# First layer's activations kept by token residue mod 4 for the strided attention groups

## The chip, the cores and the metric

The kernel runs on one core of a Trainium2 chip. The metric is the device time of one execution in microseconds (us). Three runs of the kernel before the change took 2244.28, 2245.24 and 2247.7 us; their median, 2245.24 us, is the time that the change is compared with. One further execution was profiled, and all rows of the trace shown below come from that one.

On the core, TensorE (PE) multiplies matrices: it first loads a 128x128 block as weights (PEld, the stationary operand) and then streams the columns of the other operand through it. VectorE (DVE), ScalarE (ACT) and GpSimd (POOL) work element by element on 128 partitions, and DMA queues move data; SyncE (SP) and ACT issue the DMAs of this kernel.

## The reference

Two decoder layers on 1024 tokens of width 1024, all in float32. The first layer is a dilated sliding-window attention, the second a gated linear recurrence; both also attend into 256 memory tokens and have a gate:

```python
for l in range(DEPTH):                       # DEPTH = 2
    h = rms_norm(x, norm_gain[l])
    cols = h @ w_in[l]                       # q, k, v | memory query | gate
    mix = dilated_mixer(...) if l % 2 == 0 else hgrn2_mixer(...)
    mem_out = memory_cross_attention(q_mem, mem, ...)
    y = jnp.concatenate([mix, mem_out], axis=-1) * jax.nn.silu(gate)
    x = x + y @ w_out
```

In the dilated mixer there are three groups of eight heads, (window, dilation) = (128, 1), (512, 4), (2048, 16). Each group has its own q, k and v columns. A token t of a group sees t, t - d, t - 2d and so on, with d the dilation, up to the window; the three outputs of a head are merged by their softmax denominators. A group of dilation d can be computed apart for each residue of the token number mod d.

## The kernel before

**Numbers and operands.** A float32 product is made of three TensorE passes: each operand is split into a rounded part `hi` and a rest `lo`, and the kernel adds hi·hi, hi·lo and lo·hi. So each 128x128 block of activations meets 512 columns of weights in three matmuls (lines 222 to 224 in `project`). The normed activations are held transposed in two tiles of 128 x 8 x 1024 floats, `hhi` and `hlo`: partition and block k together are the feature, and the last axis is the token, in natural order. In the projections of this layer a block of 128 tokens is the stationary operand, and the weights (`wh`, `wl`) stream.

**The stages of the first layer.** The rows of `x` are loaded in eight tiles of 128 tokens, normed, transposed and split into `hhi` and `hlo` (`put_hT`). Then follow the first half of the gate columns (`gate_chunk(0)`), the memory keys and values, the memory queries with their attention (`mem_queries`, `mem_attend`), and four gate slices for the memory part (`gate_mem`). Their results go to scratch arrays in DRAM: `gate_scr` by token rows, `om_scr` and `gatem_scr` as features by tokens. Then come the six attention steps, (Q, g) for two halves of the heads Q and the groups g = 2, 1, 0 in this order: each projects k, v and q for 8 tiles of 128 tokens and attends, with a tile's attention running beside the projections of later tiles. At the end `out_proj` reads the scratch arrays back, multiplies by the gate, and projects.

**Which tokens a tile holds.** `tile_rows` says it: group 0 takes 128 neighbouring tokens, group 1 every 4th token of a half, group 2 every 8th token of all (its dilation of 16 is met by a mask inside the tile). `lhs_group` turns this into slices of `hhi` and `hlo`, so that a weight load for group 1 reads floats at a step of 4, for group 2 at a step of 8.

**What sets the order.** The program is written step by step as above; the layer that builds the instruction streams places each engine's instructions by a simulated timeline and by the buffers that come free, so that neighbouring steps interleave on an engine. The streams are then fixed: each engine runs its own list in order and waits for semaphores. Weights are loaded in pieces by SP, copied to `wh` by ACT and to `wl` by DVE (`piece`, lines 182 and 184). Three PSUM tiles `acc` take the projections. The second-layer part, from line 847 on, is not touched.

**Lines that matter below.** Line 222 to 224: the three projection matmuls; 266 to 271: `head_norm`; 277: the transposes of q and k; 702: scores of groups 1 and 2; 708 and 710: mask, minimum and exponential; 715: transposes of the probabilities; 717: their copy `pts`; 721: products with v; 373, 438 and 410: stores to `om_scr`, `gatem_scr` and `gate_scr`; 805: the loads of the first two in `out_proj`.

## Time and profile before

| what | value |
|---|---|
| median of three runs | 2245.24 us (2244.28 to 2247.7) |
| the profiled execution, its own time | 2248.89 us |
| its span in the trace | 2247.0 us |
| PE busy | 2200.2 us, 98% of the span |
| DVE busy | 1056.9 us, 47% |
| ACT busy | 735.0 us, 33% |
| POOL busy | 504.5 us, 22% |
| data moved by DMA | 185.58 MB, 83 GB/s on average |

The profiled execution is 3.65 us longer than the median of the runs. The time line of the first layer, in us from the start of the span: norm and transposes to about 40, first gate half, memory keys and values to about 170, memory queries to 251, the six attention steps from 240 to 1225, output projection to about 1490. A busy share says how much of the time an engine had an instruction in flight; for PE, whose matmuls overlap, it is the spacing of the starts that tells how fast it runs.

### The profile page before, as it was taken

What the parts mean: (1) busy time and instruction counts of PE and PEld (TensorE: products, weight loads), DVE (VectorE), ACT (ScalarE), POOL (GpSimd) and SP (SyncE); (2) the same over time, 40 slices, a digit from 0 to 9 for tenths busy, and PEclk for the clock granted to TensorE, in tenths of its full rate; (3) what the DMA queues carried; (4) which work ended last, traced back from release to release, by engine and by line L of the source; (5) the groups of instructions that cost most, each with busy time, mean ns of one, the idle gap of its engine ahead of it and who ended that gap; (6) DMA issues with size and microseconds to landing.
All of it is one profiled execution on the core that took longest, in us unless ns stands there. A gap on an engine that the chain in (4) does not pass through costs nothing.

```text
span 2247.0 us, 29432 instructions
## 1 busy us (share of the span) xinstructions
PE 2200.2 (98%) x11288; PEld 1952.4 (87%) x11288; DVE 1056.9 (47%) x2198; ACT 735.0 (33%) x1447; POOL 504.5 (22%) x720
## 2 busy tenths in 40 slices
PE   8999999999999999999999998889999999999999
PEld 6778999999888999999988877678888888888787
DVE  5646213413424422422433559752657772776443
ACT  5436323423423322422422531232542222222211
POOL 2813212212212222222222125511200000000221
PEclk9999999999999999999999999999999999999999
DMA  5542111211211211211211286531311111112733
GB/s 192 161 141 62 52 38 43 72 38 49 66 38 46 64 43 41 69 43 43 67 43 43 72 268 197 173 101 42 90 49 50 48 60 54 57 48 66 245 121 113
DMA packets 152667, 185.58 MB, mean 83 GB/s; under 512 B 17104, under 2 KB 88016, under 8 KB 152528
## 3 DMA queue, kind: packets, MB, share of 16 engines
q1 hardware_dynamic: 115200, 140.50, 20.8%
q10 hardware_dynamic: 37328, 43.20, 5.4%
q8 instruction: 90, 1.47, 0.3%
q14 instruction: 49, 0.40, 0.1%
HBM read 140.48 MB, written 43.19 MB: 82 GB/s over the span
## 4 chain that ended last, share of the span: by engine, by line
PE 87%; DMA 5%; DVE 4%; ACT 1%; issue 1%; POOL 1%; SPq 0%; ACTq 0%; DVEq 0%; POOLq 0%
PE acc L222 16%; PE acc L224 16%; PE acc L223 16%; PE acc L422 5%; PE acc L423 5%; PE acc L424 5%; PE acc L498 3%; PE acc L496 3%; PE po L721 3%; PE acc L497 3%; PE pt L277 2%; DMA ol<-o_scr 2%; PE s L702 2%; PE pt L949 1%; PE s L949 1%; PE pt L715 1%
## 5 line engine op out<-in xcount | busy, mean ns | idle before, releaser
L222 PE MATMUL acc<-wh,hhi 128*128 128x512 f32 x1536 | 614.6, 404 | 4.4 <-DVE qn L271 1.5
L223 PE MATMUL acc<-wl,hhi 128*128 128x512 f32 x1536 | 617.8, 403 | 0.0
L224 PE MATMUL acc<-wh,hlo 128*128 128x512 f32 x1536 | 617.1, 404 | 0.0
L222 PEld LDWEIGHTS acc<-wh,hhi 128*128 128x128 f32 x1536 | 389.7, 254 | 36.4 <-DVE qn L271 1.6
L156 POOL TENSOR_TENSOR rr<-rv,nhalf 128x4 f32<-128x4 f32 (+1 forms) x152 | 147.6, 972 | 1204.9 <-DVE rv L154 1196.0
L223 PEld LDWEIGHTS acc<-wl,hhi 128*128 128x128 f32 x1536 | 390.6, 254 | 29.8 <-DVE wl L184 0.4
L224 PEld LDWEIGHTS acc<-wh,hlo 128*128 128x128 f32 x1536 | 389.8, 254 | 30.0
L184 DVE TENSOR_TENSOR wl<-raw,wh 128x1024 fp32r<-128x1024 f32 x168 | 213.1, 1269 | 403.7 <-ACT wh L147 403.1
L147 ACT ACTIVATE wh<-raw 128x1024 fp32r<-128x1024 f32 x168 | 177.7, 1059 | 216.7 <-PE acc L224 61.9
L424 PE MATMUL acc<-hhi,wl 128*128 128x512 f32 x512 | 204.1, 399 | 0.0
L423 PE MATMUL acc<-hlo,wh 128*128 128x512 f32 x512 | 203.9, 398 | 0.0
L422 PE MATMUL acc<-hhi,wh 128*128 128x512 f32 x512 | 203.1, 397 | 0.6 <-DVE ol L435 0.6
L268 DVE TENSOR_REDUCE ss<-sq 128x4 f32<-128x512 f32 x116 | 79.4, 684 | 189.1 <-ACT sq L266 188.9
L496 PE MATMUL acc<-wh,yhi 128*128 128x512 f32 x384 | 156.9, 412 | 11.5 <-DVE x L503 7.6
L497 PE MATMUL acc<-wl,yhi 128*128 128x512 f32 x384 | 154.8, 403 | 4.2 <-DVE wl L184 4.2
L498 PE MATMUL acc<-wh,ylo 128*128 128x512 f32 x384 | 153.4, 404 | 0.2 <-POOL ylo L1140 0.2
L266 ACT ACTIVATE sq<-acc 128x512 f32<-128x512 f32 x116 | 68.9, 594 | 204.3 <-PE acc L224 198.0
L710 ACT ACTIVATE pa<-pa,st 128x128 f32<-128x128 f32 (+1 forms) x192 | 84.4, 441 | 109.2 <-DVE st L708 109.2
L717 DVE COPY pts<-pt 128x256 f32<-128x256 f32 (+1 forms) x96 | 51.8, 544 | 143.8 <-PE pt L715 143.8
L271 DVE TENSOR_TENSOR qn<-acc,rr 128x512 f32<-128x512 f32 x116 | 79.2, 687 | 82.1 <-PE pt L277 47.4
L422 PEld LDWEIGHTS acc<-hhi,wh 128*128 128x128 f32 x512 | 96.3, 188 | 19.0 <-DVE ol L435 0.8
L423 PEld LDWEIGHTS acc<-hlo,wh 128*128 128x128 f32 x512 | 96.3, 188 | 18.6
(220 smaller groups left out, 3133.6 us busy)
## 6 DMA issues: line engine op xcount, KB each, us to landing
raw<-in_w_in_a_dram SPq DMA_DIRECT2D x88, 512.0 KB, 3.9
raw<-in_w_in_b_dram SPq DMA_DIRECT2D x40, 512.0 KB, 3.9
o_scr<-os ACTq DMA_DIRECT2D x48, 256.0 KB, 2.0
ol<-o_scr SPq DMA_DIRECT2D x16, 768.0 KB, 6.1
raw<-in_w_mem_kv_dram SPq DMA_DIRECT2D x16, 512.0 KB, 4.2
raw<-in_w_out_a_dram SPq DMA_DIRECT2D x12, 512.0 KB, 5.2
raw<-in_w_out_b_dram SPq DMA_DIRECT2D x12, 512.0 KB, 4.2
gt<-gateb_scr SPq DMA_DIRECT2D x24, 256.0 KB, 5.2
```

The lines of the kernel that those rows point to most:

```text
L147: A.activation(dst, src, AF.Copy)
L156: G.tensor_tensor(r[:], v[:], nhalf[:, :n], op=OP.pow)
L184: W_LO.tensor_tensor(lo[:], raw[:], hi[:].bitcast(F32), op=OP.subtract)
L222: T.matmul(ps, hi, wh[:, j, :], start=k == 0, stop=False)
L223: T.matmul(ps, hi, wl[:, j, :], start=False, stop=False)
L224: T.matmul(ps, lo, wh[:, j, :], start=False, stop=k == n - 1)
L422: T.matmul(ps[:], wh[:, k, :], mh, start=k == 0, stop=False)
L423: T.matmul(ps[:], wh[:, k, :], ml, start=False, stop=False)
L424: T.matmul(ps[:], wl[:, k, :], mh, start=False, stop=k == 7)
L496: T.matmul(pss[ch][:], hi[:, k, :], wh[:, j, :], start=k == 0, stop=False)
L497: T.matmul(pss[ch][:], hi[:, k, :], wl[:, j, :], start=False, stop=False)
L498: T.matmul(pss[ch][:], lo[:, k, :], wh[:, j, :], start=False, stop=k == 3)
```

## The change

The transposed activations are written in another order of tokens. The rows of `x` are loaded by residue: tile m now holds 128 tokens of residue m // 2 mod 4 (`residue_rows`), so that position 256 r + j of `hhi` and `hlo` is token 4 j + r. With that, a tile of group 1 is 128 neighbouring positions, and a tile of group 2 is every second position. Three things follow from the other order:

- The first gate half is stored to token rows at a step of 4. The memory output and the memory gate are features by tokens; they are stored with the residue inside each 128 tokens (`by_residue`), in runs of 32 floats, two stores for each one of before. `y_a` puts them into natural order when it splits them into hi and lo, by a strided write.
- The six attention steps run in the order (0, 2), (0, 1), (1, 2), (1, 1), (0, 0), (1, 0), so both steps of group 0 come last.
- Before the first of these two, `natural_order` rearranges `hhi` (by ACT) and `hlo` (by DVE) to natural order: eight blocks of 128x1024 each, the first two into the room of the tile `kl` that is not yet in use, the others each into the place two blocks before, and the two in `kl` back into the last two places. 20 copies in all. `ROLLED` has group 0 use the blocks in the order in which they become ready.

```diff
-    def project(pss, lhss, pieces, after=None):
+    def project(pss, lhss, pieces, after=None, order=None):
...
-                    k = 2 * i + j
-                    hi, lo = lhs(k)
+                    at = 2 * i + j
+                    hi, lo = lhs(2 * (order or range(4))[i] + j)
...
+    def by_residue(scr, r):
+        return scr.rearrange("p (a r j) -> p r a j", a=8, r=4)[:, r]
...
+        if scr is om_scr:
+            for hh in range(2):
+                r0 = (2 * hp + hh) * 128
+                SQ.dma_start(by_residue(scr[r0:r0 + 128], mp), os[:, hh].rearrange("p (a j) -> p a j", j=32))
+            return
...
+    def natural_order(spare):
+        for n, e in (("hi", A), ("lo", V)):
+            slots = [hts[n][:, k, :] for k in range(8)]
+            rooms = [spare[n, k] for k in range(2)] + slots
+            for k in range(8):
+                copy(e, rooms[k].rearrange("p (j r) -> p j r", r=4), slots[k].rearrange("p (r j) -> p j r", r=4))
+            for k in range(2):
+                copy(e, slots[6 + k], spare[n, k])
+        hts["at"] = [6, 7, 0, 1, 2, 3, 4, 5]
...
     def lhs_group(g, m):
-        r0, st = tile_rows(g, m)
-        return lambda k: (hts["hi"][:, k, r0:r0 + 127 * st + 1:st], hts["lo"][:, k, r0:r0 + 127 * st + 1:st])
+        if g == 0:
+            return lhs_natural(m)
+        if g == 1:
+            return lhs_natural(m % 4 * 2 + m // 4)
+        r0 = 256 * (m % 4) + m // 4
+        return lambda k: [hT(n, k)[:, r0:r0 + 255:2] for n in ("hi", "lo")]
+
+    def residue_rows(scr, m):
+        return rows(scr, 1, m // 2 + 4 * (m % 2))
...
-    for Q in range(2):
-        for g in (2, 1, 0):
+    group_order = (0, 2), (0, 1), (1, 2), (1, 1), (0, 0), (1, 0)
+    for Q, g in group_order:
...
-                first = Y.dma_start(xt[:], x[m * 128:(m + 1) * 128, :])
+                first = Y.dma_start(xt[:], residue_rows(x, m))
...
+            for Q, g in group_order:
+                if (Q, g) == (0, 0):
+                    t = kpool.tile([128, NT, 4, 128], F32R, name="kl")[:].rearrange("p (k m) h t -> p k (m h t)", k=4)
+                    natural_order({(n, k): t[:, 2 * i + k, :] for i, n in enumerate(("hi", "lo")) for k in range(2)})
...
-                y = y.rearrange("p (k t) -> p k t", k=4)
-                copy(A, hi[:], y)
-                V.tensor_sub(lo[:], y, hi[:].bitcast(F32))
+                y = y.rearrange("p (k r j) -> p k j r", k=4, r=4)
+                hi, lo = (t[:].rearrange("p k (j r) -> p k j r", r=4) for t in (hi, lo))
+                copy(A, hi, y)
+                V.tensor_sub(lo, y, hi.bitcast(F32))
```

**How the instructions move.** Three places are shown. The lists are those of the engines' own streams; `x3` behind a row is three of its kind in a row.

The first place is ACT at the end of the memory attention, where the attention steps begin. Here `os` is the memory output of two heads, `qn` in this place a gate slice, `sq` the squares for the first k tile. Before:

```order
L373 DMA om_scr<-os 128x2x256
L147 ACTIVATE pmh<-pt 128x4x128
L438 DMA gatem_scr<-qn 128x512
L147 ACTIVATE os<-po 128x512
L373 DMA om_scr<-os 128x2x256
L266 ACTIVATE sq<-acc 128x512 x3
L740 ACTIVATE kT<-pt,gqk 128x512 x2
```

With the change:

```order
L382 DMA om_scr<-os 1024x1x32 x2
L147 ACTIVATE pmh<-pt 128x4x128
L477 DMA gatem_scr<-qn 1024x1x32 x2
L147 ACTIVATE kl<-hhi 128x1024 x2
L147 ACTIVATE os<-po 128x512
L382 DMA om_scr<-os 1024x1x32 x2
L268 ACTIVATE sq<-acc 128x512 x3
L784 ACTIVATE kT<-pt,gqk 128x512 x2
```

The first two of the eight block copies stand here, at the very start of the attention steps and not at their fifth; each store has become two of 1024 runs of 32 floats. DVE has its two copies `kl<-hlo` at the same place.

The second place is DVE where a step of group 1 ends and a step of group 0 begins. `ISA` is the masked minimum of line 708 (749 in the changed kernel), `pts` the probabilities on their way back to PE, `wl` a weight piece. Before:

```order
L717 COPY pts<-pt 128x256
L708 ISA pa,st<-s,masks 128x128
L708 ISA st 128x1
L708 ISA pa,st<-s,masks 128x128
L708 ISA st 128x1
L268 TENSOR_REDUCE ss_4889<-sq 128x4
L154 TENSOR_SCALAR rv_4891<-ss_4889 128x4
L184 TENSOR_TENSOR wl<-raw,wh 128x1024
L268 TENSOR_REDUCE ss_4960<-sq 128x4
L154 TENSOR_SCALAR rv_4962<-ss_4960 128x4
L184 TENSOR_TENSOR wl<-raw,wh 128x1024
```

With the change:

```order
L149 COPY hlo<-hlo 128x1024 x5
L758 COPY pts<-pt 128x256
L184 TENSOR_TENSOR wl<-raw,wh 128x1024
L749 ISA pa,st<-s,masks 128x128
...
L149 COPY hlo<-hlo 128x1024
L758 COPY pts<-pt 128x256
L749 ISA pa,st<-s,masks 128x128
...
L149 COPY hlo<-kl 128x1024
L184 TENSOR_TENSOR wl<-raw,wh 128x1024
L149 COPY hlo<-kl 128x1024
```

Where rows are left out stand one more pair of minimum and read-out each time. Eight copies now stand between the attention's and the weights' rows, five of them in one block. ACT has its eight, `hhi<-hhi` and `hhi<-kl`, spread between exponentials and weight pieces.

The third place is PE at the same point, in the first k tile of the step (0, 0) of the changed kernel, with what each instruction waits for. Numbers tell tiles of one name apart: `wl_7065` is the weight piece that DVE makes behind the five copies, `wl_7569` the one between the last two.

```order
L224 MATMUL acc_7838<-wh_7063,hhi_122 128x512 [waits Activation_49]
L762 MATMUL po_7336<-vv_6935,pts_7348 128x128 [waits Activation_49]
L762 MATMUL po_7336<-vv_6935,pts_7348 128x128
L225 MATMUL acc_7838<-wl_7065,hhi_122 128x512 [waits DVE_49]
L226 MATMUL acc_7838<-wh_7063,hlo_123 128x512
L762 MATMUL po_7336<-vv_6935,pts_7363 128x128 [waits DVE_49]
L762 MATMUL po_7336<-vv_6935,pts_7363 128x128
L224 MATMUL acc_7838<-wh_7063,hhi_122 128x512 [waits Activation_49]
L225 MATMUL acc_7838<-wl_7065,hhi_122 128x512
L226 MATMUL acc_7838<-wh_7063,hlo_123 128x512
L224 MATMUL acc_7838<-wh_7567,hhi_122 128x512 [waits Activation_49]
L225 MATMUL acc_7838<-wl_7569,hhi_122 128x512 [waits DVE_49]
```

In the same place of the kernel before, the same kinds of rows stand with waits for the weight pieces alone. SP's list is the same row for row; from within the last attention step on, the lists of the other engines are the same too, so the output projection and the second layer keep their order on every engine.

More of the change, by code (lines that the diff above doesn't have):

```diff
@@ L185, in piece, with plan_chunk @@
         return v(hi[:]), v(lo[:])
-    def plan_chunk(key, w, c0, r0=0, nr=D):
+    ROLLED = (1, 2, 3, 0)
+    def plan_chunk(key, w, c0, r0=0, nr=D, order=None):
         v = w[r0:r0 + nr, c0:c0 + 512].rearrange("(k p) n -> p k n", p=128)
-        for i in range(nr // 256):
+        for i in order or range(nr // 256):
             plan.append((key, v[:, 2 * i:2 * i + 2, :]))
@@ L219, in project, with project_tiles @@
                 for j in range(2):
-                    k = 2 * i + j
-                    hi, lo = lhs(k)
-                    T.matmul(ps, hi, wh[:, j, :], start=k == 0, stop=False)
+                    at = 2 * i + j
+                    hi, lo = lhs(2 * (order or range(4))[i] + j)
+                    T.matmul(ps, hi, wh[:, j, :], start=at == 0, stop=False)
                     T.matmul(ps, hi, wl[:, j, :], start=False, stop=False)
-                    T.matmul(ps, lo, wh[:, j, :], start=False, stop=k == n - 1)
+                    T.matmul(ps, lo, wh[:, j, :], start=False, stop=at == n - 1)
             if after:
                 after(i)
-    def project_tiles(key, lhs, each):
+    def project_tiles(key, lhs, each, order=None):
         W = take(key, 4)
@@ L427, in feature_proj, with gate_slice @@
         return pss
-    def gate_slice(key, scr, pool=gs, name="os", gain=None):
+    def gate_slice(key, scr, pool=gs, name="os", gain=None, mem_a=False):
         for hf, ps in enumerate(feature_proj(key)):
@@ L437, in gate_slice @@
                 V.scalar_tensor_tensor(sg, sg, gain, ps[:], op0=OP.mult, op1=OP.mult)
-            SQ.dma_start(scr[:, hf * 512:(hf + 1) * 512], sg)
+            if mem_a:
+                for i in range(2):
+                    SQ.dma_start(by_residue(scr, 2 * hf + i), sg[:, i * 256:(i + 1) * 256].rearrange("p (a j) -> p a j", j=32))
+            else:
+                SQ.dma_start(scr[:, hf * 512:(hf + 1) * 512], sg)
     og = const.tile([128, 1], F32, name="og")
@@ new lines, in trunk_kernel, with each_k, each_v, each_q @@
+            for Q, g in group_order:
+                if (Q, g) == (0, 0):
+                    t = kpool.tile([128, NT, 4, 128], F32R, name="kl")[:].rearrange("p (k m) h t -> p k (m h t)", k=4)
+                    natural_order({(n, k): t[:, 2 * i + k, :] for i, n in enumerate(("hi", "lo")) for k in range(2)})
+                order = None if g else ROLLED
+                kT = kpool.tile([128, NT, 4, 128], F32 if g else F32R, name="kT")
+                kl = None if g else kpool.tile([128, NT, 4, 128], F32R, name="kl")
+                vv, ql = {}, {}
+                lhs = lambda m: lhs_group(g, m)
+                def each_k(m, ps):
+                    n = head_norm(ps, ap_)
+                    rotary(n, g, 1, m)
+                    t = heads_T(n)
+                    A.activation(kT[:, m], t[:], AF.Copy, scale=gqk[:, g:g + 1])
+                    if g == 0:
+                        V.scalar_tensor_tensor(kl[:, m], t[:], gqk[:, g:g + 1], kT[:, m].bitcast(F32),
+                                               op0=OP.mult, op1=OP.subtract)
+                def each_v(m, ps):
+                    vv[m] = vring.tile([128, 512], F32, name="vv")
+                    copy(A, vv[m][:], ps)
+                def each_q(m, ps):
+                    n = head_norm(ps, ap_)
+                    rotary(n, g, 0, m)
+                    t = heads_T(n)
+                    q = at_.tile([128, 4, 128], F32 if g else F32R, name="qT")
+                    if g:
+                        copy(A, q[:], t[:])
+                    else:
+                        ql[m] = at_.tile([128, 4, 128], F32R, name="ql", bufs=1)
+                        split_evac(q[:], ql[m][:], t[:])
+                    if waiting:
+                        attend(Q, g, *waiting.pop(), kT, kl, vv)
+                    waiting.append((m, q, ql.get(m)))
+                project_tiles(("k", Q, g), lhs, each_k, order)
+                project_tiles(("v", Q, g), lhs, each_v, order)
+                waiting = []
+                project_tiles(("q", Q, g), lhs, each_q, order)
+                attend(Q, g, *waiting.pop(), kT, kl, vv)
```

59 lines of the change are left out of this document (14 added, 45 removed).

## The prediction

> **What bounds the kernel now.** I read the page's shares first, then the waits of the stretch in which the change works (240 to 1225 us, the six attention steps), then the spacing of PE's matmuls there.
>
> ```profile
> PE 2200.2 (98%) x11288; PEld 1952.4 (87%) x11288; DVE 1056.9 (47%) x2198; ACT 735.0 (33%) x1447; POOL 504.5 (22%) x720
> PEclk9999999999999999999999999999999999999999
> ...
> DVE wl L184 <- ACT wh L147: 268.4, 64, 37.1
> ACT sq L266 <- PE acc L224: 175.9, 63, 6.8
> DVE pts L717 <- PE pt L715: 126.9, 51, 5.3
> PEld acc L222 <- DVE qn L271: 1.6, 3, 0.7
> PE acc L222 <- DVE qn L271: 1.5, 5, 0.4
> ```
>
> The first two lines are of the page, the others of the waits from 240 to 1225 us (who waited for whom, us in total, times, longest). ACT and DVE wait for PE for hundreds of us; PE waits for anybody for some 3 us in 985. So in these steps the time is the sum of PE's own instructions, the granted clock is full, and only what changes PE's spacing, or makes PE wait, counts. DVE, ACT, POOL and the DMAs have room, and what is added to them is free until PE waits for it.
>
> How fast PE runs differs between the groups. The weight loads of line 222 in three stretches of pure projection (820 to 860 us: group 2, step of 8; 480 to 520: group 1, step of 4; 650 to 690: group 0, neighbours):
>
> ```profile
> L222 PEld LDWEIGHTS acc<-wh,hhi 128*128 128x128 f32 x55 | 18.1, 331 | 0.0
> L222 PEld LDWEIGHTS acc<-wh,hhi 128*128 128x128 f32 x57 | 17.4, 310 | 0.0
> L222 PEld LDWEIGHTS acc<-wh,hhi 128*128 128x128 f32 x59 | 11.1, 188 | 2.4
> ```
>
> The load is the same 128x128 block; only the step between its floats differs: 331, 310 and 188 ns. The first two are never idle, the third has gaps: with steps, the load sets the pace. The same in the timeline of PE (start, duration; matmuls overlap, so the starts count), first and last row of a run for each group:
>
> ```profile
> 820.17 0.41 PE L223 MATMUL acc<-wl,hhi 128*128 128x512 f32 x1
> 829.78 0.41 PE L223 MATMUL acc<-wl,hhi 128*128 128x512 f32 x1
> ...
> 484.72 0.39 PE L222 MATMUL acc<-wh,hhi 128*128 128x512 f32 x1
> 489.65 0.40 PE L222 MATMUL acc<-wh,hhi 128*128 128x512 f32 x1
> ...
> 655.12 0.39 PE L222 MATMUL acc<-wh,hhi 128*128 128x512 f32 x1
> 659.04 0.39 PE L224 MATMUL acc<-wh,hlo 128*128 128x512 f32 x1
> ```
>
> 39 spacings of 246.4 ns, 21 of 234.8 and 17 of 230.6. Over whole steps the means of the spacings between neighbouring projections are 245.2 ns (243 to 400 us, 532 of them), 235.4 (402 to 555, 467) and 229.3 (567 to 730, 491); these I use.
>
> A second cost shows where PE returns from transposes, scores or products to a projection: the next weight load could not run ahead.
>
> ```profile
> 266.18 0.61 PE L224 MATMUL acc<-wh,hlo 128*128 128x512 f32 x1
> 266.62 0.41 PE L222 MATMUL acc<-wh,hhi 128*128 128x512 f32 x1
> ...
> 555.90 0.60 PE L222 MATMUL acc<-wh,hhi 128*128 128x512 f32 x1
> 556.34 0.40 PE L223 MATMUL acc<-wl,hhi 128*128 128x512 f32 x1
> ...
> 568.48 0.47 PE L223 MATMUL acc<-wl,hhi 128*128 128x512 f32 x1
> 568.79 0.40 PE L224 MATMUL acc<-wh,hlo 128*128 128x512 f32 x1
> ```
>
> The first projection after other work takes 0.44 us up to the next in groups 2 and 1, 0.31 in group 0. Counted in the timeline, such returns are 18 + 18 in group 2 (243 to 400 and 740 to 905 us) and 32 + 33 in group 1 (402 to 555 and 915 to 1070).
>
> **The change part by part: the gain.** Each group has two steps of three projections of 8 tiles by 8 blocks by 3 passes: 1152 matmuls. Group 1 now loads neighbours, as group 0 does: 1152 x (235.4 - 229.3) = 7.0 us, and 65 returns x 0.13 = 8.5. Group 2 loads every second float, which no row of the trace shows. One bound is the step of 1 (188 ns load): 1152 x (245.2 - 229.3) = 18.3 us and 36 x 0.13 = 4.7. The other is the step of 4 (310 ns): 1152 x (245.2 - 235.4) = 11.3 and no gain at returns. Between them decide these rows of DVE, all of 128x512: the first has all operands as neighbours, the second reads and writes floats two apart, the third reads floats three apart.
>
> ```profile
> L271 DVE TENSOR_TENSOR qn<-acc,rr 128x512 f32<-128x512 f32 x116 | 79.2, 687 | 82.1 <-PE pt L277 47.4 <-POOL rr L156 33.4 <-PE pt L715 1.3
> L923 DVE TENSOR_TENSOR z<-kk,ff 128x512 f32<-128x512 f32 x8 | 5.5, 685 | 6.5 <-PE acc L424 6.4
> L923 DVE TENSOR_TENSOR zq<-qz,ff 128x512 f32<-128x512 f32 x16 | 13.2, 846 | 0.0
> ```
>
> There a step of 2 costs nothing (685 against 687) and a step of 3 already 0.16 us; and PE's load grows by 21 ns only from 4 to 8, so its cost too comes below 4. I take the bound of the step of 1. Together 7.0 + 8.5 + 18.3 + 4.7 = 38.5 us, less 1 for returns counted in both terms: 37.5.
>
> The Trainium skill (SBUF — State Buffer, Door 1: The DMA port swizzle) agrees on the step of 2: SBUF is read in lines of 16 bytes, and two hits per line keep full speed, which two floats of a line are. But it also gives 4 floats as the step that is free, and that speaks against the change: by it group 1 would gain nothing, and the sum would lose 15.5 us. The row of 310 against 188 ns says that a step of 4 is not free; I follow the row, and keep the rule as a rival.
>
> **The rearrangement.** Each engine has ten copies: eight blocks, and two of them back out of `kl`. Two stand at the start of the steps, behind the last stores of the memory part, where the timelines of ACT and DVE show (in brackets the idle time before, and who ended it):
>
> ```profile
> 250.70 0.60 ACT L147 ACTIVATE os<-po 128x512 f32<-128x512 f32 x1 [6.07 <-PE po L370]
> 255.18 0.69 DVE L268 TENSOR_REDUCE ss<-sq 128x4 f32<-128x512 f32 x1 [9.80 <-ACT sq L266]
> ```
>
> ACT is idle for 6.07 us ahead of the last `os`, DVE for 9.80. Two copies each fit, also behind a wait for the last stores to land; queued behind them on ACT are `os` and the squares of the first k tile, which ACT waited 3 us for anyway. If they came late, PE would wait for a free `acc`; no cost.
>
> The other eight stand in the change of step from (1, 1) to (0, 0). What they cost must be bounded, since no copy of this form is in the trace. The nearest rows, by form:
>
> ```profile
> L147 ACT ACTIVATE wh<-raw 128x1024 fp32r<-128x1024 f32 x168 | 177.7, 1059 | 216.7 <-PE acc L224 61.9 <-PE acc L423 49.5 <-DMA raw<-in_w_in_a_dram 36.9
> L184 DVE TENSOR_TENSOR wl<-raw,wh 128x1024 fp32r<-128x1024 f32 x168 | 213.1, 1269 | 403.7 <-ACT wh L147 403.1
> L717 DVE COPY pts<-pt 128x256 f32<-128x256 f32 x52 | 21.9, 422 | 86.2 <-PE pt L715 86.2
> L708 DVE CUSTOM_DVE_ANT_0 pa<-s,masks 128x128 f32<-128x128 f32 x104 | 24.8, 285 | 1.8 <-PE s L699 1.2
> L708 DVE DVE_READ_ACCUMULATOR2_ANT st<- 128x1 f32 x192 | 15.9, 83 | 0.0
> ```
>
> A block of 1024 floats between neighbours takes 1.06 us (first row). Reading floats three apart made 512 of them 0.16 us longer on DVE, so 1024 would take 1.4. If every float cost what the weight load loses per float, (331 - 188) / 128 = 1.1 ns, it would be 2.2. I take 1.4, the nearest engine and kind; ends 1.06 and 2.2.
>
> Does PE wait? By the list of DVE, from the first of the five copies to `wl_7569` lie seven copies, two `wl`, two `pts` and two pairs of minimum and read-out: 7c + 2 x 1.27 + 2 x 0.42 + 4 x 0.37 = 7c + 4.9 us. The first copy may start when PE is done with blocks 0 and 1 of the last tile. By the list of PE, from there to the matmul that needs `wl_7569` stand 33 projections (x 0.23 = 7.6), 18 small matmuls (x 0.11 = 2.0, from x8 in 0.81 us at 555.09) and returns for 0.5: 10.1 us. So PE waits 7c - 5.2: 4.6 us at c = 1.4, 2.2 at 1.06, 10.2 at 2.2. Queued behind the copies on DVE are also `pts`, for which PE's products with v wait in the same stretch; they lie in the same chain and are not added. ACT has its copies between exponentials and stays ahead of DVE. In the kernel before, PE lost nothing at such a place, DVE being busy for 13.96 of 25 us:
>
> ```profile
> 550.00:575.00 25.00, 25.00 (x148) 23.63 (x148) 13.96 (x41) 13.09 (x33) 8.34 (x16) 1.00 0.37 114
> ```
>
> **The rest.** The stores in short runs: 32 DMAs of 1024 runs of 128 bytes in place of 16.
>
> ```profile
> L373 ACTq DMA_DIRECT2D om_scr<-os x8: 366/377/405, 186.1 to 251.3; - x8
> L175 SPq DMA_DIRECT2D raw<-in_w_in_b_dram x12: 367/368/368, 1682.7 to 1863.1; - x12
> DMA to landing us min/median/max: 3.5/3.8/4.3
> st_scr<-st ACTq DMA_DIRECT2D x48, 4.0 KB, 1.4
> om_scr<-os ACTq DMA_DIRECT2D x8, 256.0 KB, 2.7
> ```
>
> Issuing costs ACT 0.37 us whether the runs are few (line 373) or 1024 (line 175, 1024 runs of 512 bytes, landing in 3.8 us). 16 more issues are 6 us of ACT beside PE's work: nothing on the path. Landing lies between 2.7 us (as now) and 8 x 1.4 = 11.2 (8 times the 128 short runs of `st`); I take 4, which two buffers at a memory tile per 9.3 us (186.1 to 251.3 for 8) hide. The loads of x and the gate's store keep their runs; `y_a` writes at a step of 4 for its eight memory tiles, between 0 and 8 x 0.6 us (half of 1.1 ns by 512) of which its DMA waits hide some. I put 1 us for all of these, with 0 and 5 as ends.
>
> **The sum.** 37.5 - 4.6 - 1 = 31.9 us off the span of 2247.0, so 2215.1; the profiled execution with its 2248.89 would go to 2217, and the median, 3.65 lower, from 2245.24 to **2213 us**.
>
> **The rivals.** *A step of 2 costs like a step of 4.* For it: the load's growth between 1 and 4 has no row in between. Against: DVE's free step of 2, as said. Gain 7.0 + 8.5 + 11.3 - 0.5 = 26.3; less 5.6 it is 20.7, so 2225.
>
> *The change of step costs 2.2 us a copy.* PE waits 10.2; and if `y_a` costs its 5 too: 37.5 - 15.2 = 22.3, so 2223. For it: all floats of the source lie 1 KB apart. Against: DVE and ACT take 1 ns per float anyway, time in which a far float may be fetched.
>
> *Group 1 is slowed by its attention and not by the step*, having two key blocks where group 2 has one, so that neighbours help it nothing: 37.5 - 15.5 - 5.6 = 16.4, so 2229. This is what the skill's free step of four would give. Against it: the row of 310 ns comes from 480 to 520 us, where the windows show DVE at 0.00 of 25 us from 475 on:
>
> ```profile
> 475.00:500.00 25.00, 25.00 (x107) 25.00 (x107) 0.00 (x0) 2.99 (x5) 0.00 (x0) 1.00 0.00 1
> ```
>
> *The stores become the bound, and the kernel slower.* Its place is the memory attention, 186 to 251 us: if the two stores of a memory tile land one after the other in 11.2 us each, 22.4 us replace 9.3 for eight tiles: 8 x 13.1 = 105 us lost, 2318. It decides from 9.3 + 31.9 / 8 = 13.3 us per tile on. Against it: the 1.4 us of `st` is the time of any small store, not of its runs.
>
> The Trainium skill (DMA: Bandwidth & Descriptors, Specifications) has 512 bytes as the least size at full rate, with a read and a write back below; no run shows what that costs here, and `st`'s 32 byte runs land soonest of all.
>
> **How the numbers follow.** My forecast 0.68; step of 2 as of 4, 0.11; slow copies 0.12; group 1 unhelped 0.02; stores the bound 0.05; that some other wait, such as one at the new borders of the steps, eats nearly all of it, 0.02. The range: best case 37.5 - 2.2 = 35.3, and 3 more if group 0's own best spacing (227 at full quiet) holds: 2207; on the other side to the first two rivals with some of each: 2228. A change of 0.2% (4.5 us) is about what a measurement can tell. Faster 0.93, the same 0.02, slower 0.05.
>
> **What would show it.** In the changed kernel's profile: weight loads of line 224 at 188 ns in groups 1 and 2 and spacings near 229 ns; if group 2 shows 300 and 235, the first rival holds. Returns of 0.31 us. Copies `hlo<-hlo` of about 1.4 us, and PE waiting about 5 us in all for `wl` and `pts` at the first k tile of (0, 0). Stores to `om_scr` landing in about 4 us, with PE without a gap from 186 to 251 us. What would make it wrong: a wait that the lists don't show, or spacings that don't follow the load.

## The result and the profile after

The changed kernel takes 2221.72 us (median of 4 runs, 2220.92 to 2225.21), the kernel before 2246.47 (4 runs, 2244.28 to 2247.82): a ratio of 0.9894, 95% interval 0.9877 to 0.9911, or 24.75 us less. The forecast was 32 us less, 2213. In a later round, on the same chip as the kernels compared with it there, the changed kernel took 2227.40 us (2222.94 to 2229.22) against 2246.26, a ratio of 0.9907 (0.9892 to 0.9923). So the runs of the changed kernel spread over 8.3 us (2220.92 to 2229.22), and those of the kernel before over 9.6 (2241.49 to 2251.12). One execution of each round was profiled, with spans of 2223.2 and 2221.0 us; they are called the first and the second profile below, and the rows of this section are of the first.

The page of the changed kernel, its first line and the shares of the engines that load and multiply:

```profile
span 2223.2 us, 29472 instructions
...
PE 2173.2 (98%) x11288; PEld 1833.9 (82%) x11288; DVE 1070.7 (48%) x2208; ACT 755.8 (34%) x1457; POOL 510.7 (23%) x720
```

PE is still the bound. The weight loads (PEld) fell from 1952.4 to 1833.9 us. The same loads by line in three stretches of projection (300 to 340 us: group 2, floats two apart; 460 to 500: group 1, now neighbours; 1130 to 1170: group 0, neighbours as before):

```profile
L224 PEld LDWEIGHTS acc<-wh,hhi 128*128 128x128 f32 x56 | 10.8, 193 | 2.2
L224 PEld LDWEIGHTS acc<-wh,hhi 128*128 128x128 f32 x57 | 10.7, 188 | 2.3
L224 PEld LDWEIGHTS acc<-wh,hhi 128*128 128x128 f32 x57 | 10.7, 188 | 2.2
```

The loads are 193, 188 and 188 ns where they were 331, 310 and 188, and all three have gaps now (last column). The first projection after other work takes 0.32 us up to the next in groups 2 and 1, where it took 0.44. PE's timeline in group 2, first and last row of a run of 72 projections:

```profile
345.39 0.40 PE L225 MATMUL acc<-wl,hhi 128*128 128x512 f32 x1
361.97 0.40 PE L225 MATMUL acc<-wl,hhi 128*128 128x512 f32 x1
```

That is 71 spacings of 233.5 ns. Counted over whole steps as in the prediction, group 2 has 233.4 ns in both steps, group 1 229.8 and 229.1, group 0 229.7 and 228.9; before, they were 245.2, 235.4 and 229.3.

What took part of the gain back stands at the change from step (1, 1) to (0, 0). Waits of PE from 235 to 1205 us (us in total, times, longest), then the group rows of the copies there, then ACT's timeline and PE's:

```profile
PE acc L224 <- ACT hhi L147: 4.5, 3, 2.3
```

```profile
L147 ACT ACTIVATE hhi<-hhi 128x1024 fp32r<-128x1024 f32 x6 | 12.7, 2145 | 0.0
L149 DVE CAST hlo<-hlo 128x1024 fp32r<-128x1024 f32 x6 | 7.4, 1366 | 0.0
```

```profile
881.34 4.03 ACT L147 ACTIVATE hhi<-hhi 128x1024 fp32r<-128x1024 f32 x2
887.19 2.06 ACT L147 ACTIVATE hhi<-hhi 128x1024 fp32r<-128x1024 f32 x1
...
883.50 0.50 PE L224 MATMUL acc<-wh,hhi 128*128 128x512 f32 x1 [1.26 <-ACT hhi L147]
885.42 0.50 PE L224 MATMUL acc<-wh,hhi 128*128 128x512 f32 x1 [0.97 <-ACT hhi L147]
889.30 0.80 PE L224 MATMUL acc<-wh,hhi 128*128 128x512 f32 x1 [2.30 <-ACT hhi L147]
```

A copy of a block took DVE 1.37 us, as forecast, but ACT 2.15. PE waited three times, each time for a copy of ACT: 883.50 is the first matmul behind the first copy of the pair, 885.42 the one behind the second, 889.30 the one behind the last (887.19 + 2.06). For the weight pieces `wl` of DVE, on which the forecast had put the wait, it did not wait at all.

The windows of the same stretch (PE, PEld, DVE, ACT, POOL busy, then the granted clock) show a second loss that the forecast did not have:

```profile
880.00:885.00 5.00, 3.19 (x19) 2.20 (x16) 4.09 (x9) 5.00 (x5) 0.00 (x0) 1.00 0.61 166
885.00:890.00 5.00, 2.22 (x7) 1.37 (x8) 1.97 (x4) 5.00 (x13) 2.27 (x5) 0.82 0.30 100
890.00:895.00 5.00, 5.00 (x23) 4.71 (x22) 2.19 (x6) 5.00 (x8) 0.21 (x1) 0.50 0.02 5
```

PE was idle for 1.81 + 2.78 = 4.59 us, and behind the idle time the granted clock fell to half: in windows of 1 us it is 0.60 from 888 to 889, 0.50 up to 895, and 0.99 and 1.00 in the next two. Some 6 us of PE's work at half speed cost about 3 us more, by an estimate from that length.

### The profile page after: what moved, and what is told of

It reads as the page before. It is cut to its first block, busy times and chain, and to the rows that moved or that the text cites. A ratio compares the mean times of both kernels' runs of the same rounds, so it can differ in the third digit from the quotient of the medians.

```text
span 2223.2 us, 29472 instructions
## 1 busy us (share of the span) xinstructions
PE 2173.2 (98%) x11288; PEld 1833.9 (82%) x11288; DVE 1070.7 (48%) x2208; ACT 755.8 (34%) x1457; POOL 510.7 (23%) x720
## 3 DMA queue, kind: packets, MB, share of 16 engines
q8 instruction: 90, 1.47, 0.3%
## 4 chain that ended last, share of the span: by engine, by line
PE 88%; DVE 5%; DMA 4%; ACT 2%; issue 1%; POOL 1%; SPq 0%; ACTq 0%; POOLq 0%; DVEq 0%
PE acc L224 16%; PE acc L225 16%; PE acc L226 16%; PE acc L459 5%; PE acc L460 5%; PE acc L461 5%; PE acc L539 3%; PE po L762 3%; PE acc L537 3%; PE acc L538 3%; PE pt L279 2%; PE s L743 2%; DMA ol<-o_scr 1%; PE pt L994 1%; PE s L994 1%; PE pt L756 1%
## 5 line engine op out<-in xcount | busy, mean ns | idle before, releaser
L224 PE MATMUL acc<-wh,hhi 128*128 128x512 f32 x1536 | 603.8, 397 | 8.9 <-ACT hhi L147 5.5
L225 PE MATMUL acc<-wl,hhi 128*128 128x512 f32 x1536 | 607.3, 396 | 0.0
L226 PE MATMUL acc<-wh,hlo 128*128 128x512 f32 x1536 | 605.1, 396 | 0.0
L184 DVE TENSOR_TENSOR wl<-raw,wh 128x1024 fp32r<-128x1024 f32 x168 | 214.8, 1280 | 395.0 <-ACT wh L147 393.7
L224 PEld LDWEIGHTS acc<-wh,hhi 128*128 128x128 f32 x1536 | 291.4, 190 | 69.5 <-ACT hhi L147 6.7
L226 PEld LDWEIGHTS acc<-wh,hlo 128*128 128x128 f32 x1536 | 291.2, 190 | 58.9
L225 PEld LDWEIGHTS acc<-wl,hhi 128*128 128x128 f32 x1536 | 291.4, 190 | 57.9 <-DVE wl L184 0.4
```

Of the source, the lines that this page charges most:

```text
L184: W_LO.tensor_tensor(lo[:], raw[:], hi[:].bitcast(F32), op=OP.subtract)
L224: T.matmul(ps, hi, wh[:, j, :], start=at == 0, stop=False)
L225: T.matmul(ps, hi, wl[:, j, :], start=False, stop=False)
L226: T.matmul(ps, lo, wh[:, j, :], start=False, stop=at == n - 1)
```

## The experiments

All medians with an interval come from four or five runs beside runs of the kernel before on the same chip. Four shared one round (neighbours for every group, no rearrangement, neighbours for group 2, near reads; before: 2247.70 us, 9 runs), four the later round (the stores, the loads of x, the change once more, more rooms; before: 2246.26, 7 runs), and three were run once each (steps of 2 and 3, near copies with the wait, ACT's queue doubled; before: 2248.04).

**The gain by itself.** The kernel before, with every group loading neighbours (groups 1 and 2 then get other tokens):

```diff
     def lhs_group(g, m):
-        r0, st = tile_rows(g, m)
+        return lhs_natural(m)
```

> The kernel before with one edit: the weight loads of groups 1 and 2 read 128 neighbouring positions in place of every 4th or 8th (so these two groups compute with the wrong tokens; the amount of work and every list of instructions are the same). It measures the gross gain of the load's step alone. Theory of the prediction (the load's step sets PE's spacing, 245.2 and 235.4 against 229.3 ns, and the returns, 0.44 against 0.31 us): 37.5 us less than before, 2246 to 2209. Rival (group 1 is slow for its attention, not for the step): only group 2's 22 us, 2224. Rival (the lack of gain against the forecast is already here): 30 us or less.

Measured: 2210.01 us (2207.69 to 2212.12), ratio 0.9838 (0.9820 to 0.9855): 37.7 us less than before. Its loads, over the whole run:

```profile
L222 PEld LDWEIGHTS acc<-wh,hhi 128*128 128x128 f32 x1536 | 289.2, 188 | 64.1 <-DVE qn L271 1.6 <-ACT vb L147 1.4 <-issue 1.3
```

The forecast's gain of 37.5 us for steps of 1 everywhere is right, group 1's part in it too: its spacings are 229.8 and 229.7 ns and its returns 0.32 us, so both follow the step, not the group's attention.

**The change without the rearrangement** (group 0 then gets its tokens in the order of residues):

```diff
-                if (Q, g) == (0, 0):
+                if False:
```

> The changed kernel without the 20 block copies of the rearrangement (group 0 then computes with tokens in residue order, which is wrong). Theory: the copies make PE wait 6 us, and the granted clock of 0.50 behind the wait costs 2.5 us more, so 8 to 9 us less than the changed kernel, 2222 to 2213.5. Rival (the wait alone counts, the work is made up later): 6 us less, 2216. Rival (the copies are hidden, the wait has another cause): no change, 2222.

Measured: 2216.95 us (2215.52 to 2218.10), ratio 0.9869 (0.9853 to 0.9885), 4.8 us less than the changed kernel's 2221.72 and 10 less than its later 2227.40, both of other rounds; in the profiled executions 2214.0 against 2223.2 and 2221.0. The first of these is less than the 8 to 9 us expected, and by this median alone the rival, that only the wait counts, would fit as well; the profiles decide. The windows of the change of step:

```profile
880.00:885.00 5.00, 5.00 (x38) 4.57 (x37) 2.82 (x10) 1.80 (x7) 2.70 (x6) 1.00 0.60 204
885.00:890.00 5.00, 5.00 (x30) 4.20 (x30) 1.72 (x6) 1.97 (x6) 1.80 (x5) 1.00 0.16 53
```

No idle PE and a full clock. From the 77th to the 105th weight copy on ACT (about 825 to 1220 us), which holds the change of step and little else that differs, this kernel takes 392.0 us and the changed one 400.0 and 399.1. So the rearrangement costs 7 to 8 us in a profiled run: 4.5 of idle PE, and an estimated 2.9 and 1.7 at half clock (6.83 us of it with 1.1 idle in the first profile, 3.41 in the second); less than 1 us stays open.

**Group 2 with neighbours** (other tokens for group 2), the rest as in the change:

```diff
-        r0 = 256 * (m % 4) + m // 4
-        return lambda k: [hT(n, k)[:, r0:r0 + 255:2] for n in ("hi", "lo")]
+        return lhs_natural(m)
```

> The changed kernel with group 2's weight loads reading neighbours in place of every second position (wrong tokens for group 2, same work). Theory: group 2's spacing goes from 233.4 to 229.3 ns, 1152 matmuls, 4.7 us less, 2222 to 2217. Rival (the 4 ns belong to something else of that stretch, not to the step of 2; the load itself is 193 against 188 ns): no change in spacing, 2222.

Measured: 2219.41 us (2217.46 to 2225.49), ratio 0.9888 (0.9869 to 0.9907). The interval does not tell it from the changed kernel. The trace does: group 2's spacings go from 233.4 to 229.0 ns, which over 1152 matmuls is 5.0 us, and its span is 2215.8 us against 2221.0 and 2223.2. A step of 2 is not free.

**Steps of 2 and 3 side by side.** The kernel before, group 2 at two floats and group 1 at three (the tokens are then not those of the groups):

```diff
-        r0, st = tile_rows(g, m)
+        r0, st = ((128 * m, 1), (80 * m, 3), (96 * m, 2))[g]
```

> The kernel before, with group 2 loading floats two apart (96 tokens between tiles, not 1) and group 1 floats three apart; the tokens are then not the reference's, the work is the same. It gives the rows that were missing between a step of 1 and of 4. Forecast's view (a step of 2 is free): loads of 188 ns and spacings of 229.3 in group 2. View after the result (a step of 2 costs 5 ns of load and 4 of spacing): 193 and 233.4 in group 2; group 1 with its step of 3 then lies between 193 and 310 ns of load, and if each further 4 bytes cost alike, near 250; if only the 16 byte line counts, still 193. The time lies between the kernel before and the one with neighbours everywhere: 2214 to 2232 us.

Measured: 2225.37 us. The loads (300 to 340 us: group 2; 460 to 500: group 1) and the ends of two runs of 72 projections, first group 2, then group 1:

```profile
L222 PEld LDWEIGHTS acc<-wh,hhi 128*128 128x128 f32 x57 | 11.1, 195 | 2.1
L222 PEld LDWEIGHTS acc<-wh,hhi 128*128 128x128 f32 x56 | 14.1, 253 | 0.0
```

```profile
342.53 0.39 PE L223 MATMUL acc<-wl,hhi 128*128 128x512 f32 x1
359.04 0.39 PE L223 MATMUL acc<-wl,hhi 128*128 128x512 f32 x1
...
504.18 0.40 PE L223 MATMUL acc<-wl,hhi 128*128 128x512 f32 x1
520.85 0.39 PE L223 MATMUL acc<-wl,hhi 128*128 128x512 f32 x1
```

The runs have spacings of 232.5 and 234.8 ns; over whole steps 232.7 and 234.3. With the rows of before this gives a curve: steps of 1, 2, 3, 4 and 8 floats load in 188, 195, 253, 310 and 331 ns, and matmuls stand 229.1, 232.7, 234.3, 235.4 and 245.2 ns apart. Each float beyond the second costs the load 58 ns, up to 4, as the second expectation guessed; the spacing does not follow it. From 2 to 3 the load grows by 58 ns and the spacing by 1.6; from 1 to 2 the load by 7 and the spacing by 3.6. So the forecast's sentence that with steps the load sets the pace is not what these rows show: loads of 310 ns that start 235 ns apart overlap, and up to a step of 4 most of a longer load is hidden. What the few ns are that remain is not shown. At the returns the load does show: the first projection takes 0.32, 0.38 and 0.44 us up to the next at steps of 2, 3 and 4.

The Trainium skill (SBUF — State Buffer, Door 1: The DMA port swizzle) has lines of 16 bytes, with a penalty when fewer than two reads hit a line, and it also calls a step of 4 floats free. The loads agree with the first half (195 ns at a step of 2, 253 and 310 at 3 and 4), and 310 ns and 235.4 ns speak against the second.

**Near reads in place of far ones.** The copies of the rearrangement and the memory half's copies in `y_a` run over their floats in the order of the source, so that they read neighbours and write four apart:

```diff
-                copy(e, rooms[k].rearrange("p (j r) -> p j r", r=4), slots[k].rearrange("p (r j) -> p j r", r=4))
+                copy(e, rooms[k].rearrange("p (j r) -> p r j", r=4), slots[k].rearrange("p (r j) -> p r j", r=4))
...
-                y = y.rearrange("p (k r j) -> p k j r", k=4, r=4)
+                y = y.rearrange("p (k r j) -> p k r j", k=4, r=4)
```

> The changed kernel with the order inside each copy turned: the eight block copies, and the two operations that put the memory output into natural order, run through the source in its own order (neighbours) and write at a step of 4 floats, where they read floats 1 KB apart and wrote neighbours. The result is the same. Theory (it is the far reads that make ACT take 2.15 us a block in place of 1.06): 1.1 to 1.4 us a block, PE's wait shrinks to 1 us or less, the clock stays, 8 us less than the changed kernel: 2214. Rival (a write at a step of 4 costs what the far read did): 2.1 us a block, no change, 2222.

Measured: 2224.80 us (2221.32 to 2226.85), ratio 0.9902 (0.9885 to 0.9920), no better than the change. The theory put down for it fell (1.1 to 1.4 us a block on ACT, and a wait of 1 us or less): PE waited 4.1 us for `hhi` here too, and the rival held. Its copies:

```profile
L147 ACT ACTIVATE hhi<-hhi 128x1024 fp32r<-128x1024 f32 x6 | 12.2, 2071 | 0.0
L149 DVE CAST hlo<-hlo 128x1024 fp32r<-128x1024 f32 x6 | 6.3, 1169 | 0.0
```

On ACT it does not matter on which side the floats stand apart (2.07 against 2.15 us); on DVE writing apart is 0.2 us cheaper.

**Is it the far copies or the wait?** Far copies are those whose floats stand apart on one side. The change without the rearrangement, but with ACT copying blocks of `hhi` onto themselves, near to near, 14 times, and DVE nothing (group 0 again in the order of residues):

```diff
-        for n, e in (("hi", A), ("lo", V)):
...
-                copy(e, slots[6 + k], spare[n, k])
+        for k in (2, 2, 3, 3, 4, 4, 5, 5, 6, 6, 7, 7, 0, 1):
+            copy(A, hts["hi"][:, k, :], hts["hi"][:, k, :].bitcast(F32))
```

> The changed kernel without the rearrangement (group 0 then sees its tokens in another order); in its place ACT copies blocks of `hhi` onto themselves, neighbours to neighbours: 14 copies of 1.06 us, as long together as the ten it had (6 x 2.15 + 2 x 1.1 = 15.1), and DVE copies nothing. It keeps the wait and takes the far reads away. If the half-speed clock comes from PE's wait, PE waits 4 us or more for hhi here and the granted clock falls to 0.5 to 0.7 behind it, as in the changed kernel; if it comes from the far copies or from DVE and ACT working together, the clock stays at 1.00 although PE waits. Time near 2220 in both cases, 2 to 3 us less in the second.

Measured: 2219.08 us. Waits of PE from 860 to 915 us, and the windows:

```profile
PE acc L224 <- ACT hhi L147: 2.0, 1, 2.0
PE acc L224 <- DVE qn L273: 1.5, 1, 1.5
```

```profile
875.00:880.00 5.00, 2.96 (x18) 2.09 (x16) 2.17 (x5) 5.00 (x10) 0.10 (x1) 0.95 0.81 238
880.00:885.00 5.00, 3.50 (x13) 2.91 (x13) 1.85 (x3) 5.00 (x10) 2.40 (x5) 0.50 0.17 54
```

The idle time was 3.54 us, less than wanted, since near copies of 1.05 us pass each block on sooner, and 1.5 of it was for DVE's `qn`. The clock fell to 0.50 all the same, without a float being read apart in the copies and without a block copy on DVE. The half clock belongs to PE's idle time.

**The queue of ACT, doubled.** The copies of `hlo` on ACT too:

```diff
-        for n, e in (("hi", A), ("lo", V)):
+        for n, e in (("hi", A), ("lo", A)):
```

> The changed kernel with the eight copies of `hlo` on ACT too (the whole reference is computed). Six more far copies of 2.15 us and two near ones of 1.1 stand in ACT's queue. Theory (ACT's queue sets the end of the change of step): PE's waits there grow by 12 to 15 us and the time goes to 2234 to 2242. Rival (PE waits because SBUF is shared with DVE's copies, which are gone here): the copies on ACT get shorter, near 1.1 us, and the wait grows by less than 6 us.

Measured: 2233.28 us, 10.3 us more span than the changed kernel of the second round (2231.3 against 2221.0). The windows:

```profile
885.00:890.00 5.00, 2.91 (x11) 1.93 (x11) 1.22 (x1) 5.00 (x5) 0.00 (x0) 0.64 0.38 84
890.00:895.00 5.00, 2.66 (x6) 1.42 (x6) 1.59 (x4) 5.00 (x10) 1.02 (x1) 0.50 0.39 137
895.00:900.00 5.00, 4.09 (x10) 3.21 (x11) 1.93 (x3) 5.00 (x8) 1.47 (x4) 0.50 0.17 57
```

ACT is full for the whole time, its copies hardly shorter (2.00 us, with DVE copying nothing), PE's waits for `hhi` and `hlo` grow from 4.5 to 7.8 us, and the clock stays at half for 14 us. The copies, which did not come near 1.1 us, decide for the theory and against the rival. Its size was wrong: PE's waits grew by 3.3 us and not by 12 to 15, which alone would also fit the rival's less than 6. From the 77th to the 105th weight copy the kernel takes 405.0 us, 5 to 6 more than the changed kernel; that PE, at half clock and with other work between the copies, arrives later itself is a likely reason, not a shown one. Of the rest, most came from the start of the steps, where four copies in a row, not two, made PE wait 3.2 us for the squares of the first k tile, with the clock at 0.50 from 265.1 to 268.6 us behind the wait.

**The stores, and the loads of x.** Two kernels put these back to their form before, one at a time (every token's result is then another's):

```diff
-        if scr is om_scr:
+        if False:
...
-            if mem_a:
+            if False:
```

> The changed kernel with the memory part's stores of `om` and of its gate as before: one DMA each with long runs (the tokens of these rows land in the wrong place; the work downstream is the same). In the profile of the changed kernel 2.5 us were lost between 118 and 195 us. Theory (the doubled DMAs with 128 byte runs delay the memory part): that stretch takes as long as before and the time falls by 2 to 3 us. Rival (that stretch varies with the granted clock behind a PE wait near 125 us, since the kernel without rearrangement lost only 0.8 us up to there and the one with group 2 in neighbours gained 1.1): no difference beyond 1 us in the median.

```diff
-                first = Y.dma_start(xt[:], residue_rows(x, m))
+                first = Y.dma_start(xt[:], x[m * 128:(m + 1) * 128, :])
```

> The changed kernel with x loaded in rows of natural order (every token's result is then another's; the work is the same). The change lost 1.5 us up to the first weight copy (9.52 to 10.99 us). Theory (rows 16 KB apart make the first loads land later): the first weight copy is back at 9.5 us and the time falls by 1 to 1.5 us against the changed kernel on this chip. Rival (the start-up scatters by itself): no difference beyond 0.5 us at the first weight copy.

Measured, in one round: stores 2223.04 us (2222.13 to 2225.33), ratio 0.9892 (0.9878 to 0.9907); x 2224.23 us (2223.21 to 2224.64), ratio 0.9896 (0.9881 to 0.9910); and the changed kernel itself, for which this had been put down:

> The changed kernel once more, unchanged, on the same chip as the other runs of this call. 2220 to 2225 us; if the half-speed clock belongs to the wait for the copies, it shows again near 885 to 895 us with waits of 4 us or more; if it was chance, the clock is 1.00 there.

2227.40 us, above the range put down. In its profile, the second, PE waited 4.5 us for `hhi` again, and the clock was at 0.50 again, from 887.2 to 890.6 us: that loss was not chance. The medians of the other two are 3 to 4 us below 2227.40 and 1 to 3 above the 2221.72 of the first round: from the times nothing can be told. In the traces, the lag against before at the 29th weight copy (196 us) is +4.2 us in the first profile of the changed kernel, +1.2 in the second, +0.8 without rearrangement, -0.6 in the version below, +1.7 with the old stores and -1.3 with the old loads of x. The first weight copy starts 1.5 and 1.1 us late in the two profiles of the changed kernel, 0.9 to 1.1 late in the seven others that load by residue, and 0.5 late with the old loads. So the loads of x cost about half a us, up to 1, between what theory and rival said, and the stores none that shows. They land as forecast, though each issue took ACT 0.67 us in the median and not 0.37 (DMA issues; the last number is the median in us):

```profile
om_scr<-os ACTq DMA_DIRECT2D x16, 128.0 KB, 3.4
```

Part of the scatter is the clock again. Near 126 us, PE waits once for `qn`; the windows in which it waits and behind them:

```profile
125.00:130.00 5.00, 3.09 (x17) 2.33 (x16) 3.30 (x4) 2.93 (x4) 0.01 (x1) 1.00 0.54 156
130.00:135.00 5.00, 5.00 (x17) 3.94 (x16) 1.11 (x3) 0.36 (x1) 1.01 (x1) 0.66 0.76 209
```

This is the first profile of the changed kernel, with a gap of 1.91 us in PE ahead of the slow windows. The kernel before has a gap of 1.47 there, and its clock stays at 1.00. Over all 13 profiles the gap is between 1.34 and 1.99 us: in the four where it is 1.91 or more, a stretch of about 3.4 us at 0.50 follows, in the nine with 1.85 or less, none.

**A version with more rooms.** If the cause is ACT's queue, fewer copies in the change of step should help. Here four blocks of `hhi`, not two, are copied away early, into buffers that are free: two halves in `gs`, the rotary tables of group 2, two blocks of `kl`. Four far copies are left for ACT; DVE takes two blocks back, ACT and POOL one each, and the first tiles of group 0 take the blocks 4 to 7 first.

```diff
-    ROLLED = (1, 2, 3, 0)
+    ROLLED = (2, 3, 1, 0)
...
+        for k in range(8):
+            far(A, "hi", k, spare["hi"][k] if k < 4 else [slots["hi"][k - 4]])
+        for k in range(8):
+            far(V, "lo", k, spare["lo"][k] if k < 2 else [slots["lo"][k - 2]])
+            if k in (5, 6):
+                copy(V, slots["hi"][k - 1], spare["hi"][k - 3][0])
```

> This version computes the whole reference. Four blocks of `hhi` (in place of two) are copied into free rooms long before the change of step: two halves of `gs`, the rotary tables of group 2, two blocks of `kl`; so ACT has four far copies in the change of step in place of six, DVE brings two of the blocks back, and the first tiles of group 0 take the blocks in the order 4-7, 2, 3, 0, 1. Theory (the loss at the change of step is ACT's queue of 2.15 us copies being late, and the half-speed clock comes only behind a PE wait of several us): ACT's last far copy ends near 883 in place of 889 us, PE waits under 2 us there in place of 4.5 to 6, the granted clock stays at 1.00, and the time is that of the kernel without rearrangement plus at most 2: 2217 to 2219 us. Rival (PE is held up by the far copies themselves, because they share SBUF or the power budget with it): the copies are the same in number, the clock falls to about half for some 5 us all the same, and the time stays at 2220 to 2223. Second rival (the wait moves to DVE, which now has 10 copies): waits on DVE hlo or hhi of 3 to 5 us, 2220 to 2222.

Measured: 2220.63 us (2220.10 to 2221.79), ratio 0.9882 (0.9865 to 0.9898). All its runs lie below all of the changed kernel's on that chip (2222.94 and up); against the changed kernel's first round (2221.72) it is level. The time lies above the theory's 2217 to 2219 and within both rivals' ranges, so it does not decide; ACT's last far copy, which ended at 880.65 us, the waits and the clock do. Windows:

```profile
875.00:880.00 5.00, 4.00 (x21) 2.75 (x19) 5.00 (x15) 5.00 (x5) 4.07 (x3) 1.00 0.19 34
880.00:885.00 5.00, 3.75 (x22) 3.03 (x23) 3.47 (x8) 5.00 (x14) 1.02 (x1) 1.00 0.67 227
```

PE's idle time is halved, 1.00 + 1.25 = 2.25 us, in pieces of at most 1.5, and the clock stays at 1.00, although ACT and DVE make as many far copies in all as in the changed kernel, two of them earlier; PE's waits for DVE's copies, the second rival, do not show. From the 77th to the 105th weight copy it takes 395.0 us, 4 less than the changed kernel and 3 more than the kernel without rearrangement. It beats the kernel before by 25.6 us and is the fastest of those that compute the whole reference.

## Why the prediction was right, and where it was not

The direction and the range were right, and the gain of the loads, its largest term. The time was 8.7 us too low, 1.2 of it because the kernel before itself came out at 2246.47 and not 2245.24. By its steps:

- **Group 1, 7.0 + 8.5 us.** Right: spacings of 229.8 and 229.1 ns, loads of 188 ns, and 37.7 us in all where every group loads neighbours. The rival, that group 1 is slowed by its attention, has fallen, and with it the free step of four floats of the Trainium skill (SBUF — State Buffer, Door 1).
- **Group 2, taken at the bound of the step of 1.** The failing step is "There a step of 2 costs nothing (685 against 687) ... I take the bound of the step of 1". DVE's rows did not carry over to PE: 233.4 ns, not 229.3, so this term was 5 us too large. The value lies between the two bounds, close to the step of 1 in the loads (193 ns between 188 and 310), but two thirds of the way to the step of 4 in the spacings. The other reasoning for it, that PE's load is the pace, falls with the rows for steps of 2 and 3, and spacings that don't follow the load were one of the forecast's own signs of being wrong.
- **DVE's copies, c = 1.4 us.** The number came out (1.37), by luck: it was a near copy of ACT (1.06) with 0.32 for the step, where DVE's own near copy takes 0.72 and the step 0.65 more. PE did not wait for `wl`.
- **"ACT has its copies between exponentials and stays ahead of DVE."** This failed. Only DVE's queue was added up; ACT's was not, although PE's list, on record ahead of the forecast, has three rows there that wait for Activation, which is ACT. ACT needed 2.15 us a copy, the upper end of the bounds, and so its queue, not DVE's, was late. PE's idle time, 4.6 us, came out as forecast by chance, from another wait. Per float this is about what the forecast's upper end had from the weight load (1.1 ns a float more).
- **The copies at the start of the steps, no cost.** Right: PE waited for none of them. With four on ACT in place of two (the doubled queue) it waited 3.2 us, so the room was less than the forecast's "If they came late, PE would wait for a free `acc`; no cost" made it.
- **What the forecast lacked: the clock behind the wait.** Waits were counted at their length. The half clock behind them added an estimated 3 us in the first profile, 2 in the second. The runs with longer and shorter waits show that it comes and goes with PE's idle time, with far copies or without.
- **The rest, 1 us.** About right in what can be seen: `y_a` reads apart, 128 bytes, and does not write apart as the forecast had it (its `yhi` took 1.16 us in place of 0.63), but the output projection kept its time (197 us from the last product with v to its end, against 198); the stores landed in 3.4 us against 4 forecast; the loads of x, put at nothing, cost half a us to 1. The lag of 4.2 us in the first profile at 196 us is 1.5 at the first weight copy and, for the rest, what two more stretches of 3.41 us at half clock would cost: it holds from 96.3 to 103.1 and from 130.4 to 133.9 us there, from 97.4 to 100.8 in the kernel before.

The sum with these sizes: 37.5 - 5.0 for group 2 is 32.5, and the kernel without rearrangement lies 33.0 us below before in span (2247.0 to 2214.0). The rearrangement then costs 7 to 8 and the start-up 0 to 3, which leaves 21.5 to 25.5; the two profiles show 23.8 and 26.0, the medians 24.75 and 18.9. Of the 23.8 us in the first profile, 19.8 stand at the last product with v of the first layer; the other 4 come later, where the lists are the same but for `y_a`, and the clock is at 0.50 for 27.3 us in the kernel before and 20.5 in the changed one. Why the second round's median is that much higher is open: the clocks of its three slowest runs (0.992 to 0.994, where the others of the change have 0.991 to 0.996) don't settle it, and they left no trace.

The first rival (a step of 2 costs like 4) and the second (slow copies) each hold in part; each had been priced alone, at 2225 and 2223, near what was measured, but for other sums.

## What to carry to other kernels

Price a copy on the engine that will run it: a row of another engine is one bound more, not the price. Add up every engine's queue on which the next step waits, not one. A wait of PE costs its length only while it is short; where idle pieces add up to about 1.9 us within 3.4, add the work that runs at half clock behind it, and break the wait up or move copies ahead of it, into any buffer that is free by then. And read a matmul's pace from its spacing: from a step of 2 to one of 3 the weight load grew from 195 to 253 ns and the spacing by 1.6.

## What the runs showed of the hardware

- **The granted clock.** In the records of all 13 profiles it is 1.00 or 0.50 (a window that holds both shows a mix), and it stays at 0.50 for 3.41 us or a multiple of that. All its changes in a profile lie on one grid of 3.41 us, and PE's idle time in one cell of the grid goes with the clock of the next. Cells of the first profile, then of the second (PE, PEld, DVE, ACT, POOL busy, then the clock):

```profile
884.80:888.21 3.41, 1.52 (x5) 0.76 (x5) 1.59 (x4) 3.41 (x11) 1.02 (x1) 1.00 0.44 148
888.21:891.62 3.41, 2.32 (x8) 1.93 (x9) 0.58 (x2) 3.41 (x5) 1.46 (x4) 0.50 0.02 1
891.62:895.04 3.42, 3.42 (x18) 3.42 (x18) 2.03 (x6) 3.42 (x7) 0.00 (x0) 0.50 0.04 13
...
883.80:887.20 3.40, 1.04 (x5) 0.76 (x5) 1.28 (x3) 3.40 (x8) 2.28 (x5) 1.00 0.05 8
887.20:890.60 3.40, 3.40 (x18) 3.23 (x17) 1.17 (x6) 3.40 (x5) 0.21 (x1) 0.50 0.00 0
```

In the first profile the border at 888.21 cut the wait of 2.30 us: PE was idle for 1.89 us ahead of it and for 1.09 behind it, and two cells ran at half. In the second the whole wait lay in one cell, and one cell ran at half. Between 110 and 1250 us of the 13 profiles, every full cell with 1.60 us idle or less was followed by a full one, and each of the 11 with 1.89 or more by a half one; from 1.63 to 1.85 both happened, two halved and six not. A half cell with 0.29 us idle or less was followed by a full one, with 1.08 or more by another half one. The version with more rooms had at most 1.56 us in a cell of its change of step. The Trainium skill (TensorE: Matmul & The Clock Gate, Part 1: The HAM clock gate) has a gate with these two states, steered by PE's activity in windows of some 3.4 us, and calls an idle window of that length the cause. The lengths agree; the cause differs here, since 1.89 us idle in a window were enough.
- **POOL beside DVE's copies.** The last piece of a rotary on POOL, the same instruction a tile earlier and beside the five copies of DVE:

```profile
866.66 0.46 POOL L719 TENSOR_TENSOR qn<-t,t 128x128 f32<-128x128 f32 x1
872.16 6.12 POOL L719 TENSOR_TENSOR qn<-t,t 128x128 f32<-128x128 f32 x1
```

It ended 0.3 us after DVE's five copies did (871.80 + 6.14); in the second profile it took 6.19 us. The Trainium skill (SBUF — State Buffer, SBUF: two separate sides) has a port pair that DVE and POOL lock against each other for a whole instruction; this agrees, and here POOL did not get in between five instructions either. It cost nothing: PE's transposes of this `qn` begin at 879.85 us with no gap ahead of them. What it would cost where PE waits for the rotary is not shown.
- **Floats apart halve ACT's speed on either side**: 1024 of them, read 1 KB apart, took 2.15 us, written 16 bytes apart 2.07, and as neighbours 1.06. DVE took 1.37, 1.17 and 0.72 (the copies back out of `kl`).
